# Tree-masked attention on one core: PSUM tile of pair 46, start-up constants and first V copies rearranged

## The chip, the cores and the metric

The kernel runs on one core of a Trainium2 chip. Its time is the device time of one execution in microseconds (us). Beside the times of whole executions there is one profiled execution, with a trace of its instructions and of its DMA packets.

## The reference

Attention over 8 x 12 heads, 512 positions and 64 dimensions, with a mask in which position i sees only itself and its ancestors in a binary tree:

```python
mask = np.zeros((seq, seq))
for i in range(seq):
    mask[i, i] = 1
    parent = i
    while parent > 0:
        parent = (parent - 1) // 2
        mask[i, parent] = 1
scores = np.einsum('bhqd,bhkd->bhqk', Q, K) * scale
scores = scores + (1 - mask) * (-1e9)
weights = np.exp(scores - np.max(scores, axis=-1, keepdims=True))
weights = weights / (np.sum(weights, axis=-1, keepdims=True) + 1e-10)
return np.einsum('bhqk,bhkd->bhqd', weights, V).astype(np.float32)
```

Inputs and output are float32: 12.58 MB each for Q, K, V and the output.

## The kernel before

The 96 heads are worked through in 48 pairs (NP = 48). Two heads fill the 128 rows of TensorE's array, 64 dimensions each. Four pairs make an octet of eight heads (12 octets, NO = 12), two pairs make a quad of four heads (24 quads, NQ = 24). Octets are the unit of loading, quads the unit of storing.

For each pair i the following is done.

- `transpose(i)` (L276): TensorE turns K and Q of the pair into a PSUM tile `kqp`, K in an order of its columns that the permutation matrices `ptile` give. `evac(i)` (L302): DVE copies `kqp` to SBUF as `kq`. The pool `psT` has one buffer, so the next transposes wait for this copy.
- `scores1(i)` and `scores2(i)`: TensorE adds mask codes (L313, L335, from the constant tiles `codes`) and the products of queries with keys (L318, L342) in PSUM; ScalarE takes the exponential of either (L324, 1024 columns, and L348, 768 columns).
- `values(i)` (L363): 20 small products with V, of which column 65 gives the sum of the weights, go to the PSUM tile `ob`. The pool `psO` has one buffer.
- `norm(i)`: DVE takes reciprocals of the sums (L389) and multiplies (L392) from `ob` into an output tile `of`, which holds a quad.

The three PSUM pools use all eight banks: `s1` and `s2` two each, `kqp` two, `ob` two.

V must be copied from its loaded tile `vst` to a tile `vt` in another arrangement before `values` can use it: the top of the tree on GpSimd (`spread_top`, L225), two copies of 64 rows on DVE (`spread_leaves`, L239), and four copies of 32 rows (`spread_l7`, L254), two of them on DVE and two on ScalarE in the usual octet. In octet 0 all of L239 and L254 is done on DVE, in halves of four heads (`spread_first`).

The order on each engine is that in which the program is written; there is no scheduler. GpSimd issues the loads, which cast float32 to bfloat16 on the way, and all stores but the last quad's, in an order written out in `pool_program`. Stores stay 8 quads behind (BEHIND) the loads of their octets. The last quad's first half is stored from SP's queue after pair 46, its other two heads from SP's and ScalarE's queues after pair 47.

At the start, SP's queue issues the first K heads, the permutations and one copy of the codes, and ScalarE's queue the first Q heads and a second copy of the codes for rows 64 and up, since each head of a pair needs the codes in its own half of the rows. Twelve matmuls of zeros (`busy(12)`, L264) keep TensorE occupied until the first heads are there; DVE (L472) and ScalarE (L473) cast these. In each turn of the main loop TensorE works on the scores of pair i, the values of pair i-1 and the transposes of pair i+2.

Of the kernel before, what the change touches and what calls it, by code (L numbers as in the profile page):

```python
# [41 lines left out]
KTOP, KLOW = 8, 40  # L42
# [61 lines left out]
def _permutations():  # L104

    eye = np.eye(128, dtype=np.float32)
    return np.concatenate([eye[:, r:r + 32] for r in PERMS], axis=1)


def _run(order):  # L110
    at = [n for n in range(len(PERMS) - 3) if PERMS[n:n + 4] == tuple(order)][0]
    return slice(32 * at, 32 * at + 128)
# [3 lines left out]
def kernel(  # L116
# [7 lines left out]
    nc = tc.nc  # L124
    B, H, S, D = Q.shape
    P = nc.NUM_PARTITIONS
# [3 lines left out]
    NP = 2 * NQ  # L130

    fp32 = mybir.dt.float32
# [10 lines left out]
    perm_dram, top_dram, low_dram = (  # L143
        nc.inline_tensor(a.astype(ml_dtypes.bfloat16), name=name)
        for a, name in (
            (_permutations(), "permutations"), (top_np, "codes_top"), (low_np, "codes_low"),
        )
    )
# [11 lines left out]
    psT = ctx.enter_context(tc.tile_pool(name="psT", bufs=1, space=bass.MemoryType.PSUM))  # L160
    psO = ctx.enter_context(tc.tile_pool(name="psO", bufs=1, space=bass.MemoryType.PSUM))


    ptile = consts.tile([P, 32 * len(PERMS)], bf16)
    first = [consts.tile([P, 2, 4, D], fp32, name=f"first_{n}") for n in "kq"]
    codes = [
        consts.tile([P, a.shape[1]], bf16, name=f"codes_{n}")
        for n, a in enumerate((top_np, low_np))
    ]
    for tile_codes in codes:  # L170
        nc.vector.memset(tile_codes[:, :], 0.0)
    for eng, st, src in ((nc.sync, first[0], Kr), (nc.scalar, first[1], Qr)):
        eng.dma_start(out=st[:, :, :, :].rearrange("p h t d -> p h (t d)"), in_=src[:, 0:2, :])
    nc.sync.dma_start(out=ptile[:, :], in_=perm_dram.ap())
    for eng, half in ((nc.sync, 0), (nc.scalar, 64)):
        eng.dma_start(out=codes[0][half:half + KTOP, :], in_=top_dram.ap())
        eng.dma_start(out=codes[1][half:half + KLOW, :], in_=low_dram.ap())
    qperm = ptile[:, _run((0, 32, 64, 96))]
    perms = [ptile[:, _run(_slot_layout(t)[0])] for t in range(4)]
    k1code, q1code = codes[0][:, 0:128], codes[0][:, 128:640]  # L180
# [22 lines left out]
    qTs, kTs, kqps, obs, ets, ofs = {}, {}, {}, {}, {}, {}  # L203
# [26 lines left out]
    def tile_pair(o, p, h0, h1, first):  # L230

        c, step = VCOL[first], VCOL[first + 2] - VCOL[first]
        return vts[o % NV][p:p + 64, h0:h1, c:c + 2 * step].rearrange(
            "p h (t d) -> p h t d", t=2
        )[:, :, :, 0:D]

    def spread_leaves(o, upper, h0=0, h1=8):

        nc.vector.tensor_copy(  # L239
            out=tile_pair(o, 64 if upper else 0, h0, h1, upper),  # L240
            in_=vsts[o][64:128, h0:h1, upper:3 + upper:2, :],
        )

    def swapped(src, step):

        return bass.AP(
            src.tensor, src.offset, [list(src.ap[0]), list(src.ap[1]), [step, 2], [1, D]]
        )

    def spread_l7(copy, o, quad, h0=0, h1=8):  # L250

        slot = 2 * (quad % 2)
        lower = quad < 2
        copy(  # L254
            out=tile_pair(o, 0, h0, h1, 1)[32 * quad:32 * quad + 32] if lower
            else tile_pair(o, 64, h0, h1, 0)[32 * quad - 64:32 * quad - 32],
            in_=swapped(vsts[o][32:64, h0:h1, slot + (not lower), :], D if lower else -D),
        )

    def busy(n):  # L260

        ob = psO.tile([P, 2, 512], fp32, name="ob")
        for _ in range(n):
            nc.tensor.matmul(  # L264
                out=ob[:, 0, :], lhsT=zeros[:, 0:128], rhs=zeros[:, :], start=True, stop=True
            )
# [13 lines left out]
    def transpose(i):  # L280
        kqp = psT.tile([P, 2, 1024], bf16, name="kqp")
        kqps[i] = kqp
        for t in range(4):
            for a in range(2):
                transpose_one(kqp[:, 0, :], i, a, t, _slot_layout(t)[1], ksts, perms[t])
        for t in range(4):
            for a in range(2):
                transpose_one(
                    kqp[:, 1, :], i, a, t, [_psum_unit(4 * QPOS[t] + j) for j in range(4)],
                    qsts, qperm,  # L290
                )
# [17 lines left out]
    def scores1(i):  # L309

        sp = psS.tile([P, 2, 512], fp32, name="s1")
        for a in range(2):
            nc.tensor.matmul(  # L313
                out=sp[:, a, :], lhsT=k1code[64 * a:64 * a + 64, :],
                rhs=q1code[64 * a:64 * a + 64, :], start=True, stop=False,
            )
        for a in range(2):
            nc.tensor.matmul(  # L318
                out=sp[:, a, :], lhsT=keys(i, a, TOP),
                rhs=qTs[i][64 * a:64 * a + 64, :, :].rearrange("p t c -> p (t c)"),  # L320
                start=False, stop=True,
            )
        et = etpool.tile([P, 2, 4, 128], bf16, name="e1")
        nc.scalar.activation(  # L324
            out=et[:, :, :, :].rearrange("p a t c -> p (a t c)"),
            in_=sp[:, :, :].rearrange("p a c -> p (a c)"),
            func=AF.Exp, scale=scale,
        )
        ets[i] = et
# [23 lines left out]

    def values(i):

        obs[i] = ob = psO.tile([P, 2, 512], fp32, name="ob")
        e1, e2, vt = ets[i], e2s[i % NE], vts[(i // 4) % NV]

        def product(e, a, t, col, lo=0, hi=128, **flags):

            start_o = 65 * t + (t >= 2)
            col -= t < 2
            nc.tensor.matmul(  # L363
                out=ob[lo:hi, a, start_o:start_o + 65],
                lhsT=e[:, a, QPOS[t], lo:hi],
                rhs=vt[:, 2 * (i % 4) + a, col:col + 65],
                **flags,
            )

        for a in range(2):  # L370
            for t in range(4):
                product(e1, a, t, VTOP, start=t == 0, stop=False)
            for t in (2, 3):
                product(e2, a, t, VCOL[t], start=False, stop=False)
        for a in range(2):
            for t in (0, 1):
                product(e2, a, t, VCOL[SELF[t]], 0, 64, start=False, stop=t == 1)
                product(e2, a, t, VCOL[t], 64, 128, start=False, stop=t == 1)
# [28 lines left out]
    NO = NQ // 2  # L407
# [32 lines left out]
            if q == NQ - BEHIND + 1:  # L440
                spread_top(nc.gpsimd, NO - 1)

    def spread_first(quad, parts):

        for part in parts:
            if part < 4:
                spread_l7(nc.vector.tensor_copy, 0, part, 4 * quad, 4 * quad + 4)
            else:
                spread_leaves(0, part - 4, 4 * quad, 4 * quad + 4)

    def spread_vector(i):

        if i == 1 or i == 2:
            spread_first(1, range(3) if i == 1 else range(3, 6))
        o, step = divmod(i + 2, 4)
        if 1 <= o < NO:
            if step == 0:
                spread_leaves(o, 0)
            elif step == 1:
                spread_leaves(o, 1)  # L460
                for quad in (2, 3):
                    spread_l7(nc.vector.tensor_copy, o, quad)

    def pool_until(done, wanted):
        while done < wanted:
            next(program, None)
            done += 1
        return done
# [2 lines left out]
    steps = pool_until(0, 1)  # L471
    nc.vector.tensor_copy(out=ksts[0][:, 0:2, :, :], in_=first[0][:, :, :, :])  # L472
    nc.scalar.copy(out=qsts[0][:, 0:2, :, :], in_=first[1][:, :, :, :])  # L473
    busy(12)
    transpose(0)
    evac(0)
    for i in range(NP + 1):
        if i < NP:
            scores1(i)
            scores2(i)  # L480

            o, quad = divmod(i + 1, 4)
            if 1 <= o < NO and quad < 2:
                spread_l7(nc.scalar.copy, o, quad)
        if i == 1:
            transpose(2)
            evac(2)
            spread_first(0, range(4, 6))
        if i >= 1:
            values(i - 1)  # L490
            norm(i - 1)
        for n in (1 if i == 0 else i + 2,):
            if n < NP:
                transpose(n)
                evac(n)
        if i == 0:
            spread_first(0, range(4))
        spread_vector(i)
        if steps < NO:
            steps = pool_until(steps, min((i + 11) // 4, NO))  # L500
        else:
            steps = pool_until(steps, min(steps + 2, NO + (i - 2) // 2 - (NQ - 1 - BEHIND)))
        if i == NP - 1:
            store(nc.sync, NQ - 1, 0, 2)
# [32 lines left out]
```

## Time and profile before

| what | value |
|---|---|
| median of 8 runs | 138.38 us (137.23 to 139.12) |
| profiled execution, its own time | 137.77 us |
| its span | 135.9 us |
| busy: PE, DVE, ACT, POOL | 112.3, 104.4, 105.5, 95.4 us |
| granted TensorE clock | 0.977 |
| moved by the core's DMA queues | 32.23 MB, 237 GB/s |

The span is the time from the first to the last event of the profile; the execution's own time is 1.9 us longer. PE is TensorE's matmuls, PEld its weight loads, DVE VectorE, ACT ScalarE, POOL GpSimd, SP SyncE. DMA share is the mean busy share of the core's 16 DMA engines, and it goes over 1 where packets overlap. A queue is named by number: q0 carries what GpSimd issues, q1 what SP issues, q10 what ScalarE issues, q8 is marked as instructions.

### The profile page before, as it was taken

The page shows a single profiled execution, that of the slowest core. Times are in us where ns is not written, and L with a number is a line of the kernel's source. Part 1 is how long each engine was busy: PE and PEld are TensorE (multiplying, and loading weights), DVE is VectorE, ACT ScalarE, POOL GpSimd, SP SyncE. Part 2 cuts the span into 40 slices and gives each one's busy share as a digit, 9 for nine tenths or more (in the row PEclk, how much of TensorE's full clock was granted, in tenths as well). Part 3 has the DMA queues.
Part 4 walks back from the last instruction along what each step waited for, and adds up shares of the span by engine and source line. Part 5 has one row for each costly group of instructions (what it writes and reads, how often), then busy time and mean ns, then how long its engine had stood idle before and what let it go on. Part 6 is the DMA issues. An engine that isn't in the chain of part 4 may idle for free.

```text
span 135.9 us, 5536 instructions
## 1 busy us (share of the span) xinstructions
PE 112.3 (83%) x2412; PEld 80.1 (59%) x2412; DVE 104.4 (77%) x220; ACT 105.5 (78%) x121; POOL 95.4 (70%) x140
## 2 busy tenths in 40 slices
PE   4985968599899799998998997988997796988620
PEld 1344646478577586675776675765866565756410
DVE  6138789979779879689698798898798878898520
ACT  3245275959989889989989899799898877898800
POOL 6969959596896964984966796697497596393200
PEclk9999599999999999999999999999999999999995
DMA  3999999999999999999999999999999999999981
GB/s 106 220 185 196 198 196 197 197 196 199 196 199 231 325 199 205 347 199 199 349 204 200 326 228 197 307 248 198 282 273 198 258 300 198 245 383 390 361 319 37
DMA packets 42043, 32.23 MB, mean 237 GB/s; under 512 B 1476, under 2 KB 39076, under 8 KB 42020
## 3 DMA queue, kind: packets, MB, share of 16 engines
q0 software_dynamic: 40640, 30.68, 124.6%
q1 hardware_dynamic: 898, 0.77, 1.8%
q10 hardware_dynamic: 482, 0.44, 1.0%
q8 instruction: 18, 0.29, 0.8%
q14 instruction: 5, 0.04, 0.1%
HBM read 37.92 MB, written 12.58 MB: 372 GB/s over the span
## 4 chain that ended last, share of the span: by engine, by line
PE 41%; DVE 35%; ACT 14%; issue 6%; ACTq 0%
PE ob L363 15%; DVE of L392 9%; DVE vt L254 8%; PE kqp L276 8%; DVE vt L239 7%; DVE kq L302 7%; ACT e L324 6%; ACT e L348 5%; PE s L313 4%; PE ob L264 4%; PE s L335 4%; PE s L342 4%; PE s L318 3%; ACT vt L254 3%; DVE rec L389 3%
## 5 line engine op out<-in xcount | busy, mean ns | idle before, releaser
L324 ACT ACTIVATE e<-s 128x1024 bf16<-128x1024 f32 x48 | 49.0, 1021 | 18.2 <-PE s L318 17.5
L363 PE MATMUL ob<-vt,e 128*128 128x65 bf16 (+1 forms) x960 | 39.2, 198 | 11.1 <-DVE of L392 7.9
L363 PEld LDWEIGHTS <-e 128*128 128x128 bf16 (+1 forms) x960 | 30.9, 103 | 17.9 <-issue 6.1
L348 ACT ACTIVATE e<-s 128x768 bf16<-128x768 f32 x48 | 38.5, 801 | 0.0
L225 POOL COPY vt<-vst 32x512 bf16<-32x512 bf16 (+1 forms) x52 | 30.3, 583 | 10.3 <-DMA vst<-in_V_dram 5.5
L302 DVE COPY kq<-kqp 128x1024 bf16<-128x1024 bf16 x48 | 32.7, 682 | 5.3 <-PE kqp L276 5.3
L392 DVE TENSOR_TENSOR of<-ob,rec 128x512 f32<-128x512 f32 x48 | 33.2, 691 | 1.7
L209 POOL DMA_DIRECT2D kst<-in_K_dram x24 | 18.9, 788 | 12.4 <-DMA vst<-in_V_dram 10.2
L254 ACT COPY vt<-vst 32x1024 bf16<-32x1024 bf16 x22 | 22.8, 1036 | 1.8 <-DVE vt L239 1.6
L389 DVE RECIPROCAL rec<-ob 128x8 f32<-128x8 f32 x48 | 9.9, 207 | 16.1 <-PE ob L363 15.3
L400 POOL DMA_DIRECT2D out_dram<-of x23 | 17.6, 770 | 4.6 <-DVE of L392 4.0
L276 PE MATMUL kqp<-ptile,kst 128*64 128x128 bf16 x384 | 19.6, 222 | 1.2 <-issue 1.2
L318 PE MATMUL s<-kq 64*128 64x512 bf16 x96 | 19.0, 381 | 1.2 <-DVE kq L302 0.7
L313 PE MATMUL s<-codes 64*128 64x512 bf16 x96 | 18.9, 389 | 0.9 <-ACT e L324 0.2
L276 PE MATMUL kqp<-ptile,qst 128*64 128x128 bf16 x384 | 19.0, 221 | 0.5 <-DMA qst<-in_Q_dram 0.5
L209 POOL DMA_DIRECT2D qst<-in_Q_dram x24 | 18.2, 759 | 1.7 <-PE s L342 0.9
L342 PEld LDWEIGHTS <-kq 64*128 64x128 bf16 x384 | 16.1, 95 | 4.9 <-issue 0.4
L342 PE MATMUL s<-kq 64*128 64x96 bf16 (+3 forms) x384 | 17.9, 211 | 0.0
L335 PE MATMUL s<-codes 64*128 64x384 bf16 x96 | 16.2, 328 | 1.0
L254 DVE COPY vt<-vst 32x1024 bf16<-32x1024 bf16 (+1 forms) x30 | 15.8, 528 | 0.7
L335 PEld LDWEIGHTS <-codes 64*128 64x128 bf16 x96 | 7.7, 94 | 12.9 <-issue 6.1
L239 DVE COPY vt<-vst 64x1024 bf16<-64x1024 bf16 (+1 forms) x26 | 14.1, 541 | 0.8
(20 smaller groups left out, 60.3 us busy)
## 6 DMA issues: line engine op xcount, KB each, us to landing
out_dram<-of POOLq DMA_DIRECT2D x23, 512.0 KB, 10.5
kst<-in_K_dram POOLq DMA_DIRECT2D x23, 256.0 KB, 11.4
qst<-in_Q_dram POOLq DMA_DIRECT2D x23, 256.0 KB, 9.7
vst<-in_V_dram POOLq DMA_DIRECT2D x11, 512.0 KB, 12.6
vst<-in_V_dram POOLq DMA_DIRECT2D x2, 256.0 KB, 6.3
first_q<-in_Q_dram ACTq DMA_DIRECT2D x1, 256.0 KB, 3.7
first_k<-in_K_dram SPq DMA_DIRECT2D x1, 256.0 KB, 3.4
out_dram<-of SPq DMA_DIRECT2D x1, 256.0 KB, 4.4
```

The lines of the kernel that those rows point to most:

```text
L209: nc.gpsimd.dma_start(out=kept[o][:, h0:h0 + n, :, :].rearrange("p h t d -> p h (t d)"), in_=src[:, 8 * o + h0:8 * o + h0 + n, :],)
L225: eng.tensor_copy(out=vts[o % NV][32 * j:32 * j + 32, h0:h1, VTOP:VTOP + D], in_=vsts[o][0:32, h0:h1, UNITS[TOP + j][1], :],)
L254: copy(out=tile_pair(o, 0, h0, h1, 1)[32 * quad:32 * quad + 32] if lower else tile_pair(o, 64, h0, h1, 0)[32 * quad - 64:32 * quad - 32], ...
L276: nc.tensor.transpose(out=dst, in_=st[i // 4][:, 2 * (i % 4) + a, t, :], identity=perm)
L302: nc.vector.tensor_copy(out=kq[:, :, :, :].rearrange("p k (x y) c -> p k x (y c)", x=2), in_=src)
L313: nc.tensor.matmul(out=sp[:, a, :], lhsT=k1code[64 * a:64 * a + 64, :], rhs=q1code[64 * a:64 * a + 64, :], start=True, stop=False,)
L324: nc.scalar.activation(out=et[:, :, :, :].rearrange("p a t c -> p (a t c)"), in_=sp[:, :, :].rearrange("p a c -> p (a c)"), func=AF.Exp, s ...
L335: nc.tensor.matmul(out=sp[:, a, :, 32:128], lhsT=k2code[64 * a:64 * a + 64, :], rhs=q2code[64 * a:64 * a + 64, :].rearrange("p (t c) -> p ...
L342: nc.tensor.matmul(out=sp[:, a, :, :].rearrange("p t c -> p (t c)")[:, lo:hi], lhsT=keys(i, a, TILE2[tile2]), rhs=qTs[i][64 * a:64 * a + 6 ...
L348: nc.scalar.activation(out=e2s[i % NE][:, :, :, 32:128].rearrange("p a t c -> p (a t) c"), in_=sp[:, :, :, 32:128].rearrange("p a t c -> p ...
L363: nc.tensor.matmul(out=ob[lo:hi, a, start_o:start_o + 65], lhsT=e[:, a, QPOS[t], lo:hi], rhs=vt[:, 2 * (i % 4) + a, col:col + 65], **flags,)
L392: nc.vector.tensor_tensor(out=ofs[q][:, 2 * r:2 * r + 2, :, :], in0=vals, in1=rec[:, :, :, :].to_broadcast([P, 2, 4, D]), op=ALU.mult,)
```

## The change

Three things are changed. The values of pair 46, the last but one, go to a tile of the pool `psT` under the name `kqp` rather than to `ob`. At the start, the permutations are issued first, from ScalarE's queue ahead of Q; the codes are loaded once, from SP, and DVE copies them to rows 64 and up; nine products of zeros stand in place of twelve. The V copies of octets 0 and 1 are rearranged: all six of octet 0's first half come right after the evacuation of pair 1; of its second half two are ScalarE's, after the exponentials of pair 1, two come after the evacuation of pair 2 and two after that of pair 3. In octet 1 DVE's copies come in twos, after the evacuations of pairs 5 and 6, and ScalarE's two stand together after the exponentials of pair 4. Octets from 2 on are as before.

```diff
+    nc.scalar.dma_start(out=ptile[:, :], in_=perm_dram.ap())
     for eng, st, src in ((nc.sync, first[0], Kr), (nc.scalar, first[1], Qr)):
         eng.dma_start(out=st[:, :, :, :].rearrange("p h t d -> p h (t d)"), in_=src[:, 0:2, :])
-    nc.sync.dma_start(out=ptile[:, :], in_=perm_dram.ap())
-    for eng, half in ((nc.sync, 0), (nc.scalar, 64)):
-        eng.dma_start(out=codes[0][half:half + KTOP, :], in_=top_dram.ap())
-        eng.dma_start(out=codes[1][half:half + KLOW, :], in_=low_dram.ap())
+    for st, src, rows in zip(codes, (top_dram, low_dram), (KTOP, KLOW)):
+        nc.sync.dma_start(out=st[0:rows, :], in_=src.ap())
...
-        obs[i] = ob = psO.tile([P, 2, 512], fp32, name="ob")
+        if i == NP - 2:
+            obs[i] = ob = psT.tile([P, 2, 512], fp32, name="kqp")
+        else:
+            obs[i] = ob = psO.tile([P, 2, 512], fp32, name="ob")
...
-    def spread_first(quad, parts):
+    def spread_first(copy, quad, parts):
         for part in parts:
             if part < 4:
-                spread_l7(nc.vector.tensor_copy, 0, part, 4 * quad, 4 * quad + 4)
+                spread_l7(copy, 0, part, 4 * quad, 4 * quad + 4)
             else:
                 spread_leaves(0, part - 4, 4 * quad, 4 * quad + 4)
     def spread_vector(i):
-        if i == 1 or i == 2:
-            spread_first(1, range(3) if i == 1 else range(3, 6))
-        o, step = divmod(i + 2, 4)
-        if 1 <= o < NO:
-            if step == 0:
-                spread_leaves(o, 0)
-            elif step == 1:
-                spread_leaves(o, 1)
-                for quad in (2, 3):
-                    spread_l7(nc.vector.tensor_copy, o, quad)
+        if i == 1:
+            spread_first(nc.vector.tensor_copy, 1, (4, 5))
+        o, step = divmod(i + (2 if i > 4 else 1), 4)
+        if 1 <= o < NO and step < 2:
+            if i <= 4:
+                parts = (0, 1) if step == 0 else (2, 3)
+            else:
+                parts = (0,) if step == 0 else (1, 2, 3)
+            for part in parts:
+                if part < 2:
+                    spread_leaves(o, part)
+                else:
+                    spread_l7(nc.vector.tensor_copy, o, part)
+    def spread_scalar(i):
+        if i == 1:
+            spread_first(nc.scalar.copy, 1, (0, 1))
+        o, quad = divmod(i + 1, 4)
+        if 2 <= o < NO and quad < 2:
+            spread_l7(nc.scalar.copy, o, quad)
+        if i == 4:
+            for quad in (0, 1):
+                spread_l7(nc.scalar.copy, 1, quad)
...
-    busy(12)
+    for st, rows in zip(codes, (KTOP, KLOW)):
+        nc.vector.tensor_copy(out=st[64:64 + rows, :], in_=st[0:rows, :])
+    busy(9)
...
-            o, quad = divmod(i + 1, 4)
-            if 1 <= o < NO and quad < 2:
-                spread_l7(nc.scalar.copy, o, quad)
+            spread_scalar(i)
         if i == 1:
             transpose(2)
             evac(2)
-            spread_first(0, range(4, 6))
+            spread_first(nc.vector.tensor_copy, 1, (2, 3))
...
         if i == 0:
-            spread_first(0, range(4))
+            spread_first(nc.vector.tensor_copy, 0, range(6))
```

## The prediction

> **What bounds the kernel now.** I read the slices of the span first, then the DMA queues.
>
> ```profile
> DMA  3999999999999999999999999999999999999981
> GB/s 106 220 185 196 198 196 197 197 196 199 196 199 231 325 199 205 347 199 199 349 204 200 326 228 197 307 248 198 282 273 198 258 300 198 245 383 390 361 319 37
> q0 software_dynamic: 40640, 30.68, 124.6%
> q8 instruction: 18, 0.29, 0.8%
> ```
>
> The DMA engines are busy from the second slice to the last but one. The rate has two levels: about 197 GB/s while fp32 inputs are written as bf16, and about 390 GB/s while outputs are written. Nothing lies between them but mixtures, so the engines never run out of work for long. At these rates 18.87 MB of loaded bf16 take 96 us and 12.58 MB of output take 32 us, together 128 us of a span of 135.9. No compute engine is above 83%. Next come the stages of the end (columns: busy time of each engine, granted clock, DMA share, GB/s):
>
> ```profile
> 118.00:127.00 9.00, 7.67 (x172) 5.42 (x169) 7.85 (x15) 8.37 (x11) 5.21 (x8) 1.00 1.07 379
> 127.00:131.00 4.00, 1.88 (x50) 1.51 (x46) 1.81 (x5) 1.56 (x2) 0.76 (x1) 1.00 0.95 357
> 131.00:132.00 1.00, 0.00 (x0) 0.00 (x0) 0.00 (x0) 0.00 (x0) 0.00 (x0) 1.00 0.58 210
> 132.00:133.00 1.00, 0.00 (x0) 0.00 (x0) 0.00 (x0) 0.00 (x0) 0.00 (x0) 1.00 0.75 255
> 133.00:134.00 1.00, 0.00 (x0) 0.00 (x0) 0.00 (x0) 0.00 (x0) 0.00 (x0) 0.51 0.10 34
> ```
>
> Compute ends near 131, DMA near 133.8. Is the last stretch only the latency of the last small stores, or a backlog? The mean share can't tell; the completion records of the trace can. Every transfer posts one completion per DMA engine. GpSimd's last store, issued at 127.31, completes at 130.46 to 130.88 on seven engines, at 131.14 to 132.00 on seven and at 132.81 and 132.82 on two. The last two small stores, issued at 131.00, complete near 133 on fourteen engines and at 133.9 to 134.2 on two. The packets that end after 133.1 come alternately from two series, each 43 ns apart without a hole. So **two slow DMA engines** are still behind with old work when the last store comes; they set the end. After them the span has 1.7 us left, and the execution 1.9 us more.
>
> How they fell behind: in the first transfers the completions of one load lie 0.65 us apart. After the first 16 KB packet of q8 (14.77 us, 0.96 us long) one engine is 1.57 us behind the first, and every further packet of q8 adds some 0.9 us to an engine; at 120 us the slowest is 3.9 us behind the first.
>
> The chain of waits at the end (start, duration, engine, line):
>
> ```profile
> 127.31 0.79 PE L363 MATMUL ob<-vt,e 128*128 128x65 bf16 x20
> 127.76 0.81 ACT L348 ACTIVATE e<-s 128x768 bf16<-128x768 f32 x1
> 128.14 0.21 DVE L389 RECIPROCAL rec<-ob 128x8 f32<-128x8 f32 x1 [1.12 <-PE ob L363]
> 128.38 0.69 DVE L392 TENSOR_TENSOR of<-ob,rec 128x512 f32<-128x512 f32 x1
> 129.22 0.78 PE L363 MATMUL ob<-vt,e 128*128 128x65 bf16 x20 [1.12 <-DVE of L392]
> 130.28 0.69 DVE L392 TENSOR_TENSOR of<-ob,rec 128x512 f32<-128x512 f32 x1
> 131.00 0.39 ACTq L400 DMA_DIRECT2D out_dram<-of  x1
> ```
>
> Pair 47's values wait for pair 46's normalization, because both use the one `ob`.
>
> **What the Trainium skill says.** In the Trainium skill, "DMA: Bandwidth & Descriptors", section "Issuing engines are not separate DMA queues", says that transfers from all issuers share the same sixteen engines; the stretch after 129 us, where three queues' packets interleave, agrees. The same page, "Why a DMA increments its semaphore by 16 and not by 1", says that a transfer uses the largest number of engines up to 16 that divides its slowest dimension: 8 engines for the 8 rows of `codes_top`, 10 for the 40 of `codes_low`. The records show 8 and 10 completions from the engines. "Runtime: NRT & Kernel Launch", "Instruction fetch mechanics", has instructions refilled in blocks of 16 KiB, 256 of them, over a DMA queue: q8's 18 packets fit TensorE's 4824 matmuls and weight loads. "Perfetto Trace Analysis", "What 'DMA-bound' means", lists single DMA engines as a bound: the reading above.
>
> **The change, part by part,** against the profiled execution's 137.77 us, which lies 0.61 under the median of 138.38.
>
> *Pair 46 into `kqp`.* The last transposes (pair 47) end at 124.4 and their evacuation at 125.6, so the tile is free when values(46) start at 127.31; that start stays, since scores of pair 47 hold it. Values(47) no longer wait for 129.07. Four products need only the first exponential (done 127.86), the fifth needs L348, done 128.57. From there 16 of 20 products, 0.78 x 16/20 = 0.63 us, end at 129.25; DVE is free since 129.07. Normalization starts at 129.3 for 130.04: 0.7 us less on the compute chain. Two small stores are issued 0.7 us sooner; SP, ScalarE's queue and GpSimd have nothing else then. On the two slow engines these packets (8 KB each from either store, 16 x 43 ns = 0.69 us) still stand behind the same backlog: 0. On the other fourteen the hole of 131 to 132 shrinks, which ends nothing. I take **0**; bounds 0 and -0.7.
>
> *Permutations first, fewer warm-up products.* Nine for twelve, 5.17/12 = 0.43 each, end at 5.69 for 6.98. The permutations leave on ScalarE's queue at 0.73 rather than SP's at 1.23. Q moves behind them, 0.54 later (issue 0.73 to 1.27), so its cast (0.62) ends at 5.6 for 5.09; the warm-up covers that. The first exponential, at 8.77 before, starts 1.2 to 1.3 sooner. Should Q's load or the granted clock be late, this shrinks towards 0.
>
> *Codes.* Two DMAs and their issues (0.60 and 0.29 on ScalarE's queue) go; on SP both codes move up one place. Two DVE copies are added, not in the trace; nearest row L254 at 32x512, 282 ns at least and 439 in the mean, so 0.6 to 0.9. They stand ahead of the first evacuation of `kqp` and wait for the codes, complete by 5.83 before and about half a microsecond sooner now: done near 6.2, while that evacuation waits for the transposes until about 6.3. Cover gone, 0.5 us of the 1.2. For the DMA engines 50 KB are gone: 8 packets of 1.28 KB and 40 of 1 KB, on one of the ten engines at most 4 x 46 + 55 = 0.24 us. Half of the engines lie 0.45 us back at 9 us, about twice that.
>
> *V copies.* Octet 0's leaves go ahead of the third evacuation (2 x 0.35), eating part of the 1.2. Two copies go from DVE (2 x 0.44) to ScalarE, where the nearest row is L473's 0.62: 1.24 together. Octet 1's copies only change places; ScalarE's two stand together, 2.1 us, with exponentials of pair 5 behind them and TensorE's scores of pair 6 waiting on those. ScalarE has 18.2 us of idle before L324, most of it early. Net at pair 8: between +1 late and -2 early; I take -1.
>
> *Where the early time goes.* Loads don't follow it. Their order on GpSimd is the same, a load waits about 10 us in the queues after its issue, and the last V load (issued 105.00, 12.6 us to landing) arrives at 117.6. DVE starts on it at 117.99. So of an early microsecond at most 0.35 is left there; the rest becomes a wait for V. It then meets the same slow engines: 0.
>
> Sum: 0 (start) + 0 (end) - 0 to 0.24 (fewer code packets, full only if a slow engine is one of the ten). I take -0.15: 137.6 on the profiled one, **138.2** on the median.
>
> **Rivals.** *Compute sets the end* in the usual run. The 8 times spread over 1.9 us, about two of the 0.9 us refills, so their places seem to vary; where the slow engines have one refill less they end near 133.2, with the others, and the last stores count. Then 0.7 + 0.35 can go, up to 1.05 with the codes within it: 137.3 to 137.7. Against it: the median run is longer than the profiled one, as with more backlog, not less. *Slower:* one refill more on the slowest engine. The place is q8, the price 0.9 us, and it decides as soon as that engine has one more of the 18 than before; TensorE's stream is shorter by three products and their weight loads, so blocks meet the engines at other moments. Then 138.38 - 0.15 + 0.9 = 139.1. For it: lags at 120 us are far from even. Against it: 18 blocks stay 18, and a median over runs evens places out. *The change does nothing on chip:* the order of instructions on each engine does change as described, so only the saving can fail, which is the likeliest case anyway.
>
> **Numbers.** What a measurement of this kernel tells from no change is about 0.5%, 0.69 us. DMA engines bind, 0 to 0.3 off: 0.59. Compute binds: 0.27, mostly beyond 0.69. One refill more: 0.14, mostly beyond it too. With the edges shared out: faster 0.28, same 0.60, slower 0.12. The likeliest case alone is 138.0 to 138.5. The range to 8 in 10 takes most of the faster case and the nearer part of the slower one: 137.4 to 138.8.
>
> **What would show it.** Right: first exponential near 7.5; values(47) start before the normalization of pair 46 ends; last stores issued near 130; DVE or GpSimd waiting for V late; yet the end of DMA activity moves by under 0.3 us, with GpSimd's last store still completing near 132.8 on its slowest engines. Wrong: a span shorter by 0.7 or more with the same completions of that store, or DMA idle in the middle of the span.

## The result, and the profile after

The changed kernel runs in 137.57 us (median of 18 runs, 137.05 to 138.36), the kernel before beside it on the same chip in 138.54 (53 runs, 137.23 to 140.2). The ratio of runs is **0.9956, 95% interval 0.9934 to 0.9978**: 0.61 us less, 0.30 to 0.91. The ratio leaves out runs more than 1.5% above the fastest of the same kernel; the medians here and below are over all runs. The profiled execution took 137.34 us for 137.77, its span is 135.57 us for 135.86. A repeat (e6 below) gave 0.9965 (0.9942 to 0.9987).

From the page of the changed kernel, the DMA rows of the 40 slices and two of the queues:

```profile
DMA  4999999999999999999999999999999999999991
GB/s 143 183 164 196 198 196 198 197 199 195 198 196 219 339 199 205 343 203 201 339 213 199 318 238 197 291 265 198 268 288 196 248 310 198 233 375 382 373 349 49
...
q0 software_dynamic: 40640, 30.68, 125.0%
q8 instruction: 19, 0.31, 0.8%
```

The picture is the one of before: two levels of rate, no hole, and one 16 KB refill more (19 for 18). The stages of the end, changed kernel (from and to, length, busy time of PE, PEld, DVE, ACT and POOL, clock, DMA share, GB/s):

```profile
118.00:127.00 9.00, 7.55 (x157) 5.11 (x151) 7.55 (x15) 7.99 (x10) 5.66 (x8) 1.00 1.07 374
127.00:131.00 4.00, 1.68 (x44) 1.30 (x40) 1.80 (x4) 1.26 (x2) 0.76 (x1) 1.00 0.99 363
131.00:132.00 1.00, 0.00 (x0) 0.00 (x0) 0.00 (x0) 0.00 (x0) 0.00 (x0) 1.00 0.97 347
132.00:133.00 1.00, 0.00 (x0) 0.00 (x0) 0.00 (x0) 0.00 (x0) 0.00 (x0) 1.00 0.45 159
133.00:134.00 1.00, 0.00 (x0) 0.00 (x0) 0.00 (x0) 0.00 (x0) 0.00 (x0) 0.50 0.14 49
```

The hole of 131 to 132 is filled (0.97 for 0.58): the last stores come sooner. What is moved there is missing a microsecond later (0.45 for 0.75), and the tail from 133 to 134 is no shorter. The chain that feeds it, from the timeline of the changed kernel:

```profile
127.00 0.79 PE L366 MATMUL kqp<-vt,e 128*128 128x65 bf16 x20
127.00 0.76 POOL L403 DMA_DIRECT2D out_dram<-of  x1 [3.21 <-DVE of L395]
127.45 0.81 ACT L347 ACTIVATE e<-s 128x768 bf16<-128x768 f32 x1
127.72 0.29 PE L366 MATMUL ob<-vt,e 128*128 128x65 bf16 x4
127.83 0.21 DVE L392 RECIPROCAL rec<-kqp 128x8 f32<-128x8 f32 x1 [1.12 <-PE kqp L366]
128.07 0.69 DVE L395 TENSOR_TENSOR of<-kqp,rec 128x512 f32<-128x512 f32 x1
128.31 0.67 PE L366 MATMUL ob<-vt,e 128*128 128x65 bf16 x16 [0.30 <-ACT e L347]
129.02 0.21 DVE L392 RECIPROCAL rec<-ob 128x8 f32<-128x8 f32 x1 [0.26 <-PE ob L366]
129.99 0.38 ACTq L403 DMA_DIRECT2D out_dram<-of  x1
```

Values(47) start while pair 46 is still being normalized, four products first and sixteen when the exponential is there. The last store goes out at 129.99 for 131.00, one microsecond sooner, and yet the last completion of any transfer is at 134.31 for 134.20. **The DMA engines end no sooner.** The start, first from the timeline of the kernel before, then from that of the changed one:

```profile
6.91 0.41 PE L276 MATMUL kqp<-ptile,kst 128*64 128x128 bf16 x8
...
7.16 0.39 PE L276 MATMUL kqp<-ptile,qst 128*64 128x128 bf16 x8
...
8.77 1.02 ACT L324 ACTIVATE e<-s 128x1024 bf16<-128x1024 f32 x1 [3.69 <-PE s L318]
```

```profile
3.96 0.52 DVE L494 COPY codes<-codes 8x640 bf16<-8x640 bf16 x1
...
4.63 0.55 DVE L494 COPY codes<-codes 40x512 bf16<-40x512 bf16 x1 [0.16 <-DMA codes<-codes_low]
...
5.76 0.64 PE L275 MATMUL kqp<-ptile,kst 128*64 128x128 bf16 x8
...
6.19 0.63 PE L275 MATMUL kqp<-ptile,qst 128*64 128x128 bf16 x8
...
8.05 1.02 ACT L323 ACTIVATE e<-s 128x1024 bf16<-128x1024 f32 x1 [2.99 <-PE s L317]
```

The first exponential stands at 8.05 for 8.77. This varies among executions: 7.04 to 8.47 in the traces of the changed kernel, e3, e5, e6 and e8, which start alike, and 8.20 to 8.77 in those of the kernel before, e1, e2, e4 and e7.

**Where the profiled difference is.** The span ends 1.26 us after the last completion, for 1.66 before. In between the trace has, on SP, a row of semaphore instructions in which the program waits for its DMAs' completions. The profile doesn't count these as busy, so no view of the page has them; here are the times in us at which they start:

```
before  last completion 134.20 | SP: 131.41 131.47 134.21 134.28 134.34 134.40 134.46 134.52 134.58 134.64 134.71 134.76 | span 135.86
after   last completion 134.31 | SP: 130.40 130.47 130.53 130.59 133.15 133.21 133.27 133.66 134.32 134.38 134.45 134.50 | span 135.57
```

Each step of the row takes 0.06 us even when its transfer has long been done. The row is in the order of the semaphores, not of the transfers. Before, the last of the three final stores to complete is waited for third, and nine steps are still to be taken: 0.57 us from the last completion to the end of the row. After, it is ninth, three steps are left, and it takes 0.20. From the end of the row to the end of the span it is 1.10 and 1.06 us. The stores' places moved because the program deals out eight semaphores in turn to the DMAs of SP's and ScalarE's queues, as the traces name them. Before, seven such DMAs at the start leave the eighth, first and second to the final stores; the change issues two fewer (the second copy of the codes), which leaves the sixth, seventh and eighth. That is **0.37 us that no step of the prediction had.**

### The profile page after: what moved, and what is told of

The parts are those of the page before. It is cut to its first block, busy times and chain, and to the rows that moved or that the text cites. A ratio compares the mean times of both kernels' runs of the same rounds, so it can differ in the third digit from the quotient of the medians.

```text
span 135.6 us, 5534 instructions
## 1 busy us (share of the span) xinstructions
PE 111.8 (82%) x2409; PEld 80.0 (59%) x2409; DVE 104.6 (77%) x220; ACT 106.6 (79%) x123; POOL 95.3 (70%) x140
## 4 chain that ended last, share of the span: by engine, by line
PE 45%; DVE 37%; ACT 8%; issue 5%; ACTq 0%
PE ob L366 17%; DVE of L395 10%; DVE vt L253 10%; PE kqp L275 9%; DVE kq L301 7%; DVE vt L238 5%; PE s L312 5%; ACT e L323 4%; PE s L317 4%; DVE rec L392 4%; PE s L341 3%; ACT e L347 3%; PE s L334 3%; PE ob L263 3%; ACT vt L253 2%
## 5 line engine op out<-in xcount | busy, mean ns | idle before, releaser
L366 PE MATMUL ob<-vt,e 128*128 128x65 bf16 (+1 forms) x940 | 38.1, 198 | 9.0 <-DVE of L395 6.5
L395 DVE TENSOR_TENSOR of<-ob,rec 128x512 f32<-128x512 f32 x47 | 32.5, 692 | 1.6
L253 ACT COPY vt<-vst 32x1024 bf16<-32x1024 bf16 (+1 forms) x24 | 24.0, 1001 | 1.3 <-DMA vst<-in_V_dram 1.0
L275 PE MATMUL kqp<-ptile,qst 128*64 128x128 bf16 x384 | 19.5, 223 | 1.7 <-DMA qst<-in_Q_dram 1.7
L341 PE MATMUL s<-kq 64*128 64x128 bf16 (+3 forms) x384 | 17.8, 209 | 0.5 <-issue 0.4
L275 PEld LDWEIGHTS <-qst 128*64 128x64 bf16 x384 | 14.0, 113 | 2.2 <-DMA qst<-in_Q_dram 2.2
L275 PEld LDWEIGHTS <-kst 128*64 128x64 bf16 x384 | 13.0, 113 | 3.8 <-issue 2.5
```

The lines of the kernel that those rows point to most:

```text
L253: copy(out=tile_pair(o, 0, h0, h1, 1)[32 * quad:32 * quad + 32] if lower else tile_pair(o, 64, h0, h1, 0)[32 * quad - 64:32 * quad - 32], ...
L275: nc.tensor.transpose(out=dst, in_=st[i // 4][:, 2 * (i % 4) + a, t, :], identity=perm)
L341: nc.tensor.matmul(out=sp[:, a, :, :].rearrange("p t c -> p (t c)")[:, lo:hi], lhsT=keys(i, a, TILE2[tile2]), rhs=qTs[i][64 * a:64 * a + 6 ...
L366: nc.tensor.matmul(out=ob[lo:hi, a, start_o:start_o + 65], lhsT=e[:, a, QPOS[t], lo:hi], rhs=vt[:, 2 * (i % 4) + a, col:col + 65], **flags,)
L395: nc.vector.tensor_tensor(out=ofs[q][:, 2 * r:2 * r + 2, :, :], in0=vals, in1=rec[:, :, :, :].to_broadcast([P, 2, 4, D]), op=ALU.mult,)
```

## Experiments

The theories, with a letter for each. **D**: the DMA engines bind, and the slowest of them sets the end. **C**: the compute chain sets the end (the prediction's rival). **W**: formed on seeing the trace after; the gain is the place of the last stores in SP's row of waits. The first four kernels ran together (before: 138.21 us, 43 runs), the next four (138.26, 62 runs) and the last three (138.16, 35 runs) likewise.

**e1, the PSUM tile alone**, on the kernel before:

```diff
-        obs[i] = ob = psO.tile([P, 2, 512], fp32, name="ob")
+        if i == NP - 2:
+            obs[i] = ob = psT.tile([P, 2, 512], fp32, name="kqp")
+        else:
+            obs[i] = ob = psO.tile([P, 2, 512], fp32, name="ob")
```

> The kernel before with pair 46's values in the transposes' PSUM tile, and nothing else of the change. If the slow DMA engines set the end: within 0.1% of before, although the last stores are issued about 0.7 us sooner. If compute sets the end: 0.5% faster (0.7 us). If the gain of the whole change lies in the start: no change here either.

Measured: 138.11 us, ratio 0.9990 (0.9966 to 1.0013). From its timeline:

```profile
129.70 0.39 ACTq L403 DMA_DIRECT2D out_dram<-of  x1
```

The last store is 1.3 us sooner than before; the last completion is at 134.29 (before 134.20), and the row ends at 134.86, still 0.57 behind it. Of the 1.3 us, 0.7 are the edit's: the last store follows GpSimd's last one by 2.99 us for 3.69. The other 0.6 were there already at GpSimd's last store (126.71 for 127.31), in a part of the program that e1 doesn't touch, and show how far two executions differ. The PSUM part by itself changes nothing that can be measured, as D says and C denies.

**e2, the order of the waits alone**, on the kernel before: six 64-byte transfers, so that the last stores use other semaphores. They are written at pair 20, but SP's queue had nothing to wait for and issued them between 2.5 and 5.6 us.

```diff
+        if i == 20:
+            for n in range(6):
+                nc.sync.dma_start(out=spare[0:1, 32 * n:32 * n + 32], in_=perm_dram.ap()[0:1, 0:32])
```

> The kernel before with six DMAs of 64 bytes from SP's queue at pair 20 (into a spare tile that nothing reads), so that the last three stores get the completion semaphores that the end of the program waits for last (lanes 5, 6, 7, as in the changed kernel) and not the first ones (7, 0, 1). If the order of the waits at the end is part of the gain: 0.3 to 0.4 us shorter, 0.2 to 0.3%. If the gain is in DMA bytes or in compute: no change, or slower by under 0.1 us.

Measured: 137.87 us, 0.9979 (0.9955 to 1.0003). In the trace the last completion is at 134.31, the end of the row at 134.51, 0.20 behind it. The interval of the time just includes no gain. In the spans, which are what this edit should shorten, the difference is clearer: 0.31 us less in the mean (22 runs and 43 of the kernel before; 95% interval 0.1 to 0.5).

**e3, the changed kernel with the stores put back to early places** (three such transfers, issued between 2.0 and 2.6 us):

```diff
+        if i == 20:
+            for n in range(3):
+                nc.sync.dma_start(out=spare[0:1, 32 * n:32 * n + 32], in_=perm_dram.ap()[0:1, 0:32])
```

> The changed kernel with three such DMAs of 64 bytes, so that its last stores get lanes 0, 1, 2. If the order of the waits at the end is part of the gain: 0.3 to 0.4 us longer than the changed kernel, so 0.9985 of before instead of 0.9956. If not: still 0.9956 of before.

Measured: 138.35 us, 1.0010 (0.9983 to 1.0037). Last completion 134.51, end of the row 135.01. The whole gain is gone. It lost 0.6 to 0.75 us against the two measurements of the changed kernel, where the row accounts for 0.30 (0.50 for 0.20). The intervals are wide enough to hold that difference, but the spans hint at more: e3's median span is 136.55 us for 136.30 before, though its row is shorter by 0.07. Whether the three transfers, which fall among the first loads, cost time of their own, or the rest of the change does, no run tells. So e3 says that the gain can be lost through the last stores' semaphores, and not what the rest of the change is worth (+0.14 us of the time before, -0.23 to +0.51, if the transfers cost nothing). W rests on e2, in which no work of the program is changed and the span falls by about what the row gives, on e3, which goes the other way, and on the row in every trace (table below).

**e4, one load more**, on the kernel before: 4 heads of K, 256 KB as bf16, to a tile that nobody reads.

```diff
+            if o == 5:
+                for n in range(1):
+                    nc.gpsimd.dma_start(
+                        out=more[n][:, :, :, :].rearrange("p h t d -> p h (t d)"), in_=Kr[:, 0:4, :]
+                    )
```

> The kernel before with one load of four K heads more from GpSimd (256 KB of input) among those of octet 5, into a tile that nothing reads. If the DMA engines bind throughout: about 1.35 us longer, 1.0%, the spacing of the completions of such loads in the trace. If compute binds: no change that can be measured, since compute has its own data as before.

Measured: 139.76 us, 1.0108 (1.0074 to 1.0142), +1.5 us. 256 KB at the 197 GB/s of the loads are 1.33 us. Stages of its end:

```profile
131.00:132.00 1.00, 0.19 (x8) 0.08 (x6) 0.73 (x2) 0.00 (x0) 0.00 (x0) 1.00 1.00 369
132.00:133.00 1.00, 0.00 (x0) 0.00 (x0) 0.17 (x1) 0.00 (x0) 0.00 (x0) 0.71 0.81 303
133.00:134.00 1.00, 0.00 (x0) 0.00 (x0) 0.00 (x0) 0.00 (x0) 0.00 (x0) 0.50 0.90 313
```

What is added to the DMA engines in the middle comes out at the end in full, as DMA work after 132 that was not there before (0.90 for 0.10 from 133 to 134). Compute ends 1.2 us later too, since the loads behind the added one are later, so this run alone does not tell D from C.

**e5, the changed kernel with pair 46 back in `ob`** (e1's edit reversed), and **e6, the changed kernel once more**:

> The changed kernel with pair 46's values back in their own PSUM tile, so that the last stores are issued some 0.7 us later again. If the slow DMA engines set the end: as the changed kernel within 0.1%. If compute sets the end: 0.5% slower than the changed kernel, about as before.

> The changed kernel once more, so that the others of this call can be set against it on one chip. Every theory: 0.9956 of before, within its interval of 0.9934 to 0.9978.

Measured: e5 137.62 us, 0.9961 (0.9940 to 0.9981); e6 137.69 us, 0.9965 (0.9942 to 0.9987). Without the PSUM part the gain is the same, though e5's last stores go out at 130.51 for 129.98 (3.69 us after GpSimd's last, for 2.99). e5 also tells of the start. Its timeline:

```profile
5.18 0.41 PE L275 MATMUL kqp<-ptile,kst 128*64 128x128 bf16 x8
5.43 0.39 PE L275 MATMUL kqp<-ptile,qst 128*64 128x128 bf16 x8
...
7.04 1.02 ACT L323 ACTIVATE e<-s 128x1024 bf16<-128x1024 f32 x1 [1.85 <-PE s L317]
```

With the same code at this place, its first exponential is 1.0 us ahead of the changed kernel's profiled execution and 1.7 ahead of before. GpSimd's last store is issued at 126.83; in e1, whose first exponential is at 8.73, at 126.71. The start's lead does not arrive at the end.

**e7, a stall in the middle**, on the kernel before: five copies on DVE at pair 20.

```diff
+        if i == 20:
+            for _ in range(5):
+                nc.vector.tensor_copy(out=idle[:, :], in_=zeros[:, :])
```

> The kernel before with five DVE copies of 128x512 more at pair 20, 1.5 to 2.5 us on DVE's own queue, ahead of a normalization. If the DMA engines bind throughout: no change, 0.999 to 1.001. If compute binds from the middle to the end: 1.5 us or more longer, 1.1%.

Measured: 139.58 us, 1.0104 (1.0069 to 1.0138): D's expectation failed. A line of the kernel before, then timeline and stages of e7:

```profile
127.31 0.76 POOL L400 DMA_DIRECT2D out_dram<-of  x1 [3.21 <-DVE of L392]
```

```profile
62.21 2.51 DVE L488 CAST idle<-zeros 128x512 f32<-128x512 bf16 x5
...
128.29 0.76 POOL L401 DMA_DIRECT2D out_dram<-of  x1 [3.21 <-DVE of L393]
```

```profile
127.00:131.00 4.00, 2.69 (x56) 1.88 (x54) 1.80 (x4) 2.50 (x4) 0.76 (x1) 1.00 0.87 327
131.00:132.00 1.00, 0.15 (x8) 0.04 (x4) 0.77 (x2) 0.00 (x0) 0.00 (x0) 1.00 0.91 330
132.00:133.00 1.00, 0.00 (x0) 0.00 (x0) 0.13 (x1) 0.00 (x0) 0.00 (x0) 0.71 0.24 86
133.00:134.00 1.00, 0.00 (x0) 0.00 (x0) 0.00 (x0) 0.00 (x0) 0.00 (x0) 0.50 0.82 274
```

Of 2.5 us of stall one microsecond is left at GpSimd's last store against the profiled execution of before (128.29 for 127.31), and 1.6 us against e1, e2 and e11, which have no stall either (126.71 to 126.78): the compute chain makes up 0.9 to 1.5 us in 65, no more. The span's median is 1.0 us longer (137.2 for 136.2). So the end does follow the chain here.

By which stores it follows, the trace does not settle. Between 3 and 131 us there are fewer than 12 packets in flight during 1.0 us, most of it near 129 (0.25 before, 0.26 at most in the other kernels except e9). The bytes still to be moved at 120 us are 4.80 MB, within the 4.65 to 4.89 of kernels without stall or added load, so the DMA engines are not behind until then. This points to engines that run short of stores at the end. But the profiled execution has the shortest span of e7's nine: its last completion, at 134.88, is no later than e6's (134.98), and its GpSimd store completes on the slowest engine at 133.86, for 132.82 before and 133.64 in e6 and e11.

The time rises by more than the span, 1.3 us in the medians; that rest lies outside the span, where the kernel before too has runs with over 3 us.

**e8, a stall at the very end**, on the changed kernel: four copies on DVE ahead of the last normalization.

```diff
+        if i == NP - 1:
+            for _ in range(4):
+                nc.vector.tensor_copy(out=idle[:, :], in_=zeros[:, :])
```

> The changed kernel with four DVE copies of 128x512 more ahead of the very last normalization, which start the last two stores about 1.3 us later than in the changed kernel. If the slow DMA engines set the end: under 0.3 us longer, as there are 0.7 us of old packets in front of these and about 0.7 us from the issue of the last two stores that the change gave. If compute sets the end: 1.3 us longer, 0.9%.

Measured: 137.80 us, 0.9957 (0.9934 to 0.9980), no loss. Its timeline:

```profile
129.15 1.80 DVE L394 CAST idle<-zeros 128x512 f32<-128x512 bf16 x4
...
131.83 0.38 ACTq L407 DMA_DIRECT2D out_dram<-of  x1
```

The last two stores go out 1.8 us later than in the changed kernel's profiled execution. 1.4 of this is the stall (4.35 us after GpSimd's last store, for 2.99); 0.5 was there before it. So the backlog covers a delay of the last two stores alone by 1.4 us. In e7 they went out at 132.16, a little later than here, and the stores ahead of them came late as well. Whether e7's loss lies in these or in the last two is not shown.

**e9 and e10, one engine or all**, on the changed kernel: eight loads of 17 rows of 1 KB (e9), or of 16 (e10).

```diff
+        if i == 8:
+            for n in range(8):
+                nc.sync.dma_start(out=spare[0:17, 256 * n:256 * n + 256], in_=Kr[0:17, n, :])
```

> The changed kernel with eight more loads of 17 rows of 1 KB from SP's queue in the turn of pair 8, to a tile that nobody reads: 136 KB. The DMA page's rule (the largest number of engines up to 16 that divides the slowest dimension) puts all 17 rows of a load on one engine. Slowest engine sets the end: 8 x 17 packets of 1 KB at some 43 ns, the spacing of packets in the last stores, are 5.8 us more on that engine; if it is one of the leading ones, which are 2 to 3 us ahead of the slowest, 3 us of that show, otherwise up to 5.8: 140.5 to 143.5 us. Average load sets the end: 136 KB at 390 GB/s, 0.35 us: 138.0. Compute sets the end: nothing until a buffer is late: 137.6.

> The same eight loads with 16 rows of 1 KB: 128 KB, one packet of each load on each of the 16 engines. Slowest engine and average load agree here: 8 x 43 ns = 0.34 us on every engine: 137.9 to 138.0 us. Against the run with 17 rows, which moves 6% more bytes, the slowest-engine reading wants 2.5 us or more of difference, the average-load reading 0.02 us.

Measured: e9 141.92 us, 1.0262 (1.0209 to 1.0316); e10 137.69 us, 0.9959 (0.9936 to 0.9982). Six per cent more bytes cost 4.2 us. The page of e9, and its waits (what waited for what: us in all, times, longest):

```profile
GB/s 99 231 194 188 122 193 144 181 161 182 197 196 198 297 252 200 283 267 196 278 271 198 276 273 200 268 280 198 265 289 196 259 290 200 252 392 384 318 284 34
```

```profile
POOL vt L225 <- DMA vst<-in_V_dram: 14.1, 6, 4.1
```

SP's queue had nothing to wait for and issued these loads in the first 6 us. By the rule of the Trainium skill, "DMA: Bandwidth & Descriptors", section "Why a DMA increments its semaphore by 16 and not by 1", 17 rows go to one engine, since no number from 2 to 16 divides 17. The trace agrees: of the loads whose first engine completes between 18 and 21 us, fifteen engines complete within 0.7 us, and the sixteenth is 5.4 us behind the first (7.2 at most, in the loads just before). A load is complete when its last engine is, so every load came late: the rate falls to 122 and 144 in the fifth and seventh slice, GpSimd waits 14.1 us for V in all (8.6 in the changed kernel), and the last store goes out at 135.81 for 129.99. **A backlog on one engine works through the landing of the loads, on the compute chain, not only at the last store**; the time is within the range expected, by a wider road than the expectation named. e10's 0.34 us is too small to be seen here.

**e11, the codes alone**, on the kernel before: codes loaded once and copied by DVE, with two 64-byte transfers that leave the last stores at their places.

```diff
-    for eng, half in ((nc.sync, 0), (nc.scalar, 64)):
-        eng.dma_start(out=codes[0][half:half + KTOP, :], in_=top_dram.ap())
-        eng.dma_start(out=codes[1][half:half + KLOW, :], in_=low_dram.ap())
+    for st, src, rows in zip(codes, (top_dram, low_dram), (KTOP, KLOW)):
+        nc.sync.dma_start(out=st[0:rows, :], in_=src.ap())
...
+    for st, rows in zip(codes, (KTOP, KLOW)):
+        nc.vector.tensor_copy(out=st[64:64 + rows, :], in_=st[0:rows, :])
```

> The kernel before with the codes loaded once and copied by two DVE copies, twelve products of zeros and the order of issues else as before; two 64-byte DMAs on SP's queue at pair 20 keep the last stores on the same places in the row of waits as before. DMA engines bind: 50 KB less, 0.1 to 0.24 us: ratio 0.9983 to 0.9993, and some 0.0 if the slowest engines are not among the ten. Order of the waits at the end: unchanged, last wait about 1.6 us before the span's end as before, so no gain from that side; the whole of the change's gain here (0.996) would speak against it. Time outside the span: if the second copy of the codes on ScalarE's queue makes the occasional long values, no run lies more than 2.0 us above its span.

Measured: 138.11 us, 0.9993 (0.9967 to 1.0018). The point is at the small end of what D gave, and the interval holds zero. No run lay more than 2.1 us above its span, where the kernel before, beside it, had up to 3.2 (8 of 35 runs over 2.2).

The ends of the profiled executions together (us): when the last store was issued, when the last transfer completed, and how long the row of waits went on.

| kernel | last store issued | last completion | row ends after it | span |
|---|---|---|---|---|
| before | 131.00 | 134.20 | 0.57 | 135.86 |
| e1 | 129.70 | 134.29 | 0.57 | 135.93 |
| e11 | 130.47 | 134.68 | 0.57 | 136.32 |
| e3 | 130.03 | 134.51 | 0.50 | 136.07 |
| e2 | 130.47 | 134.31 | 0.20 | 135.58 |
| changed | 129.99 | 134.31 | 0.20 | 135.57 |
| e5 | 130.52 | 134.47 | 0.20 | 135.74 |
| e6 | 130.37 | 134.98 | 0.20 | 136.25 |
| e8 | 131.83 | 134.68 | 0.20 | 135.96 |

The second column runs over 2.1 us with no trace of it in the third. The third varies by 0.8 among executions, and the fourth is 0.50 to 0.57 or 0.2, by the place of the last stores alone; e4 and e7 (0.57 both, places as before) and e9 and e10 (0.14 and 0.20, places as in the changed kernel) fit in.

**Outside the span.** The row is the span's share of the gain, and there is another. Beside e6, the kernel before takes 138.34 us in the mean of its 62 runs, for 137.76: of these 0.58 us, 0.24 are in the span and 0.35 outside it. The share outside comes mostly from long runs. The kernel before took more than 2.2 us outside its span in 36 of the 140 runs of the three batches; the kernels with the changed start (the changed one, e3, e5, e6, e8, e9 and e10) did so in none of 122. Which part of the change does this, no run isolates: e11, with the codes alone, has none in 14, but neither has e1, which starts as before; e2 has 3 in 22, e4 one in 6, e7 4 in 9. The traces give a lead, no more. The last 16 KB packet of q8, the 19th, starts after the end of the span in e2, e4, e7 and e11, and inside it in e1 and with the changed start (e8 and the kernel before have only 18 in their traces). The only long run with a trace is e7's: there the packet starts at 138.81, 2.3 us after the span has ended, in an execution of 139.5 us.

## Why the prediction was right, and where it was wrong

It forecast no change that can be measured as the likeliest case, at 138.2 us, and a DMA-bound end that the edits don't reach. The ratio puts the kernel at 138.38 x 0.9956 = 137.77: inside the range, at -0.61 us for a sum of -0.15, just inside the 0.5% that it called no change. The mechanism was right for the parts it looked at; the gain came from two places it had left out. That the sum came out as near as this is in part luck: the interval, 0.30 to 0.91, goes beyond 0.69. By its number alone the rival that compute sets the end, 137.3 to 137.7, was nearer than the main case's 138.2; e1 and e5 speak against it, not the time.

- **Pair 46 into `kqp`: right.** Products in two pieces as described, the last stores near 130, worth 0 (e1: -0.14 us with an interval across zero; e5: no loss without it). The edit's own gain on the chain is the 0.7 forecast (2.99 us from GpSimd's last store to the last one, for 3.69); the 1.0 in the profiled pair has 0.3 from ahead.
- **Permutations, warm-up: the term was mis-sized.** 1.2 to 1.3 us at the first exponential became 0.72 in the profiled pair. The transposes started 1.15 sooner but took 0.64 and 0.63 us for 0.41 and 0.39, with pairs of products 0.107 us apart for 0.055. The prediction named a late clock as what would shrink this; the granted clock reads 1.00 in that stretch in both, so the cause is not in that record. In e5 the faster spacing was there by 5.18, and the first exponential 1.7 us sooner than before. The term is worth nothing at the end in either case.
- **Codes: right in kind, early in time.** The two copies took 0.52 and 0.55, 1.07 together, above the 0.6 to 0.9 estimated. They were done at 5.18 all the same, a microsecond ahead of the 6.2 named, since the codes were there sooner and K's cast ended at 3.93. The 0 to 0.24 us of DMA work is consistent with e11, and not resolved by it.
- **V copies: right.** ScalarE's two took 1.25 us together for 1.24, and at the first exponential of pair 8 the profiled execution is 1.2 us ahead (31.90 for 33.11), where 1 was taken.
- **Where the early time goes: right.** GpSimd and DVE wait for the last V load in the changed kernel's timeline, where the lead ends:

```profile
117.91 0.42 DVE L238 COPY vt<-vst 64x1024 bf16<-64x1024 bf16 x1 [0.64 <-DMA vst<-in_V_dram]
...
117.94 2.91 POOL L224 COPY vt<-vst 32x512 bf16<-32x512 bf16 x4 [2.81 <-DMA vst<-in_V_dram]
```

  DVE gets there 0.08 us sooner than before, and GpSimd's last store goes out 0.31 sooner, within the 0.35 allowed. Even this is no more than executions differ by: the traces of the changed kernel, e3, e5, e6, e8 and e10 have it at 126.83 to 127.48, those of the kernel before, e1, e2 and e11 at 126.71 to 127.31. That store's slowest engine completed at 133.10 for 132.82, where 132.8 was named.
- **What lies behind the last completion: the step that was wrong.** "After them the span has 1.7 us left, and the execution 1.9 us more", the prediction says, and takes both as fixed. The 1.7 held a row of waits of which 0.37 us depend on which semaphores the last stores have, and removing two DMAs at the start moves that. It is all or nearly all of the difference in spans (0.3 in the profiled pair and in the medians of e6, 0.2 to 0.45 in those of e5, e8 and e10). The 1.9 stands for a time outside the span that is longer in a quarter of the runs of the kernel before and in none of the changed start; that gives about as much again in the means, and its cause is open.
- **The rivals.** *Compute sets the end* in its form (a sooner chain is a sooner end) is refuted by e1 and the table. But e7 shows that it is close: with 2.5 us of stall in the middle, the end comes a microsecond later. The prediction treated the DMA engines' backlog as a cushion of any thickness; it covers a delay of the last two stores by 1.4 us (e8), and not a whole chain that arrives 1.0 to 1.6 us late (e7). *One refill more* happened in the profiled execution (19 for 18) and did not cost 0.9: completions at the end moved by 0.1. Where a refill falls may decide; this wasn't tried.

What stays open: what makes the long times outside the span, and which part of the change ends them; why e3's span is longer than that of before; and through which stores e7's stall reaches the end.

## What to carry to other kernels

Before an edit is priced at a DMA-bound end, ask from both sides: e1 and e8 show that the last two stores can move by 0.7 us one way and 1.4 the other for nothing, e7 that a stall in the middle costs a microsecond of the span all the same, and only a perturbation tells how near the two limits stand. Look also at what the program does after its last transfer: the waits at its end are taken in a fixed order, and having the last stores waited for late saved 0.3 to 0.4 us of the span where the compute edits saved nothing that could be seen. Compare spans and times apart, since a gain can lie in either: here it lay in both, and only one part is explained. Take a difference of half a microsecond between two single executions for chance until others show it. Loads whose rows do not spread over the engines can cost far more than their bytes: 136 KB on one engine cost 4.2 us.

## What the runs showed of the hardware

- A wait on a completed DMA semaphore takes SP 0.06 us, and this program's end has twelve such steps in a row: 0.14 to 0.57 us after the last completion, by their order.
- The spacing of TensorE's products halves at a moment that differs among executions of the same start: by 4.9 us in e5, near 5.9 in e9 and after 6.5 in the changed kernel, with the granted clock at 1.00 in the records of that stretch.
- One DMA engine that fell up to 7.2 us behind the first made the whole kernel 4.2 us longer (e9); at 50 us it is still 3.7 us behind.
